# A two-layer hybrid trunk on one core: mixed keys copied one product ahead, projections spread evenly over the levels, LayerNorm sums from additions, activations written in place

## The chip, the cores and the metric

The kernel runs on one core of a Trainium2 chip. The metric is device time in microseconds, the median of several executions. A profile shows one execution: what each engine did and when. The engines are named PE (TensorE, matmul), DVE (VectorE), ACT (ScalarE), POOL (GpSimd) and SP (SyncE, which issues most DMAs). Each engine works through its own queue in order; semaphores hold an instruction until what it needs is done.

## The reference, cut to what matters

Two layers are run over 1152 tokens: 128 context tokens and 1024 latent tokens. Each sub-layer is modulated, its output is gated and added to the scaled input, and a LayerNorm follows.

```python
# layer 0: attention beside a short gated convolution, then ConvFFN
# layer 1: HGRN2, a gated linear recurrence in both directions, then ConvFFN
x = layer_norm(ALPHA * x + gate * sublayer(x * (1 + scale) + shift))

def _hgrn_mixer(h, w_in, lb, norm_g, w_out, s_fw, s_bw):
    q, i, g, f_fw, f_bw = split(h @ w_in, 5)             # 8 heads of 128
    f = lb + (1 - lb) * sigmoid(f_raw)                   # decay; k = 1 - f
    # S_t = diag(f_t) S_(t-1) + k_t v_t ; o_t = q_t S_t, forward and backward
    o = rms_norm(o_f + o_b, norm_g) * silu(g)
    return o @ w_out, S_f, S_b

def _conv_ffn(h, w_up, conv_w, w_down):
    u = _dwconv(h @ w_up, conv_w)
    a, gt = split(u, 2)
    return (silu(gt) * a) @ w_down                       # 1024 -> 2 x 2816 -> 1024
```

All of it is float32.

## The kernel before, in words

Every large product is made from three fp32r products (`mm3`, L91 to L93): each operand is split into a rounded part and a remainder. `wraw` loads a weight of 128 x 1024; `wsplit` makes `whi` on ScalarE (L106) and subtracts to get `wlo`, on GpSimd unless another engine is named (L107). Activations are kept the same way, feature rows by tokens, in `hT` (two tiles of four feature blocks for each part; `Halves`). The tokens are nine tiles of 128 (t = 8 down to 0) or three chunks of 384 (c = 2, 1, 0).

From the output projection of layer 0 on, the order on every engine is the order in which the program is written; only semaphores between engines move anything.

**Feed-forward.** `ffn_up` makes 44 products (tile `psu`) with a convolution behind each on ScalarE and VectorE (L973 to L979) and stores the result to DRAM. At the last one it splits the first two weights of the down phase (`dws`) and the first two loaded activations (`split_s`). `ffn_down` works in groups of four feature blocks. The last group is made for whole token tiles (`psw`, three buffers of two banks): gate (L1173), addition (L1174), `ln_stats` (two `bn_stats` of 512 columns, an aggregate, a power on GpSimd, a scaling pass on ScalarE), and what a `tail` function adds: `tail1` the two affine passes of the output (L267 on VectorE, L268 on GpSimd), `tail0` the transposition into the next layer's `hT` by `ln_out` (four pieces of two feature blocks for each chunk). `ln_sums`, used in the output projection of the recurrence so far, gets the mean from an addition that also sums and the variance from a square on ScalarE.

**Recurrence.** Head by head. Its projections (input i, gate g, two decays f, query q; 24 steps each, one step being the three products of one feature block with 384 tokens, tile `psp`) are a generator, `projections`, out of which `fill(n)` takes n steps wherever it is called, so that TensorE has work between the steps of the scan. ScalarE evacuates them. The scan is a tree of seven levels over three chunks, 21 items (`level`):

```python
km = wtile("km")
nc.scalar.copy(km..., scan_ap(X, KBF, KBB, c * 384, 384, hh))      # mixed keys
for q3 in range(3): mm(ps..., km..., scan_ap(X, QAB, QAF, c0, P, hh))
# X *= the neighbour's total: one half on GpSimd, one on VectorE (L1364)
# new totals (L1370); copy_predicated of ps into sT (L1372), both on VectorE
```

`X` holds keys and queries of both directions, four arrays over all tokens; a level multiplies it in place. After each `level`, `fill(4)` is called (3 in head 0, 2 in head 7). Then come the states (six `fill(2)`) and the outputs (`fill(4)` three times and `fill(8)`); `upto` completes a projection that is needed, and `at["last"]` holds `fill` back from running too far ahead. Head 7 has no next head: behind its last projection come `early` products, the first three heads' part of the output projection (`pse`), for which outputs of earlier heads are loaded from DRAM (`og_load`) and split (`og_split`, L1457 and L1458). `out_unit` splits the weights of the other five heads, and `recurrence_out` makes the rest (`psd`), with `ln_sums`; it also loads and splits the first two weights of the second feed-forward (`ffn_raws`, `ffn_splits`).

## Time and profile before

| | us |
|---|---|
| median of 3 runs | 3557.26 (3554.27 to 3560.13) |
| the profiled execution, its time | 3557.42 |
| the profiled execution, its span | 3555.6 |
| TensorE busy | 3293.2 |
| VectorE busy | 1927.1 |
| GpSimd busy | 1255.0 |
| ScalarE busy | 1130.9 |

The span is from the first to the last instruction; the time holds 1.8 us more. A busy row gives for each engine the time, the share of the span and the number of instructions. A row of the waits reads "who <- for whom: us in total, times, longest". A row of instruction groups reads "line, engine, operation, tiles written <- read, shape, count | busy us, mean ns of one | idle us before them <- what ended it". A row of the timeline begins with start and length in us.

### The profile page before, as it was taken

What the parts mean: (1) busy time and instruction counts of PE and PEld (TensorE: products, weight loads), DVE (VectorE), ACT (ScalarE), POOL (GpSimd) and SP (SyncE); (2) the same over time, 40 slices, a digit from 0 to 9 for tenths busy, and PEclk for the clock granted to TensorE, in tenths of its full rate; (3) what the DMA queues carried; (4) which work ended last, traced back from release to release, by engine and by line L of the source; (5) the groups of instructions that cost most, each with busy time, mean ns of one, the idle gap of its engine ahead of it and who ended that gap; (6) DMA issues with size and microseconds to landing.
All of it is one profiled execution on the core that took longest, in us unless ns stands there. A gap on an engine that the chain in (4) does not pass through costs nothing. (4 is left out here: it accounts for less than half of the span.)

```text
span 3555.6 us, 45061 instructions
## 1 busy us (share of the span) xinstructions
PE 3293.2 (93%) x18215; PEld 3033.1 (85%) x18215; DVE 1927.1 (54%) x2667; ACT 1130.9 (32%) x1845; POOL 1255.0 (35%) x833
## 2 busy tenths in 40 slices
PE   7999999999999999988988888888789999999995
PEld 6998887799999988778887888787679999998884
DVE  6787886489973233564445454555742222233358
ACT  4314985232222231134333333333233222224111
POOL 6711333244312121423444444434423431112144
PEclk9999999999999999999999999999899999999998
DMA  7151002245552232321101111111302222223231
GB/s 203 50 154 36 1 1 79 70 128 167 166 148 62 82 126 89 116 77 67 58 20 50 46 46 30 35 52 54 123 13 84 86 86 69 62 82 126 95 120 62
DMA packets 261393, 286.39 MB, mean 81 GB/s; under 512 B 18132, under 2 KB 198560, under 8 KB 261185
## 3 DMA queue, kind: packets, MB, share of 16 engines
q1 hardware_dynamic: 260384, 281.88, 25.9%
q8 instruction: 144, 2.36, 0.3%
q0 software_dynamic: 800, 1.63, 0.2%
q14 instruction: 65, 0.52, 0.0%
HBM read 228.45 MB, written 55.02 MB: 80 GB/s over the span
## 5 line engine op out<-in xcount | busy, mean ns | idle before, releaser
L107 POOL TENSOR_TENSOR wlo<-wraw,whi 128x1024 fp32r<-128x1024 f32 x199 | 489.1, 2461 | 1307.0 <-ACT whi L106 1273.6
L91 PE MATMUL psu<-h,whi 128*128 128x388 f32 (+1 forms) x1488 | 509.5, 343 | 18.5 <-ACT psd L243 11.2
L92 PE MATMUL psu<-h,whi 128*128 128x388 f32 (+1 forms) x1488 | 509.4, 342 | 2.9 <-POOL h L386 2.9
L93 PE MATMUL psu<-h,wlo 128*128 128x388 f32 (+1 forms) x1488 | 507.8, 341 | 0.0
L974 DVE SCALAR_TENSOR_TENSOR cv<-psu,fcw,cv 128x1158 f32<-128x1158 f32 x88 | 125.2, 1423 | 529.8 <-ACT cv L973 529.8
L91 PE MATMUL psp<-h,whi 128*128 128x384 f32 x960 | 354.5, 369 | 5.4 <-ACT h L293 4.6
L92 PE MATMUL psp<-h,whi 128*128 128x384 f32 x960 | 330.7, 345 | 2.1 <-POOL h L294 2.1
L93 PE MATMUL psp<-h,wlo 128*128 128x384 f32 x960 | 331.1, 345 | 0.0
L973 ACT ACTIVATE cv<-psu,fcw 128x1158 f32<-128x1158 f32 x88 | 108.1, 1229 | 695.2 <-PE psu L93 695.2
L91 PEld LDWEIGHTS psu<-h,whi 128*128 128x128 f32 x1488 | 282.1, 190 | 20.3 <-ACT psd L243 11.4
L106 ACT ACTIVATE whi<-wraw 128x1024 fp32r<-128x1024 f32 x206 | 215.5, 1050 | 253.5 <-PE psd L93 86.1
L1358 PE MATMUL pss<-X,km 128*128 128x128 f32 x1008 | 168.3, 306 | 131.2 <-ACT km L1355 121.3
L1358 PEld LDWEIGHTS pss<-X,km 128*128 128x128 f32 x1008 | 139.5, 200 | 172.4 <-ACT km L1355 143.5
L92 PEld LDWEIGHTS psu<-h,whi 128*128 128x128 f32 x1488 | 282.0, 190 | 4.4 <-POOL h L386 3.9
L93 PEld LDWEIGHTS psu<-h,wlo 128*128 128x128 f32 x1488 | 281.6, 189 | 0.0
L91 PE MATMUL psd<-whi,s 128*128 128x512 f32 x648 | 256.5, 396 | 5.9 <-DVE cv L975 5.9
L1364 POOL TENSOR_TENSOR X<-X,tot 128x384 f32<-128x384 f32 x144 | 177.3, 1232 | 237.7 <-PE pss L1358 212.6
L92 PE MATMUL psd<-wlo,s 128*128 128x512 f32 x648 | 256.4, 396 | 0.0
L93 PE MATMUL psd<-whi,s 128*128 128x512 f32 x648 | 256.3, 396 | 0.0
L170 DVE SCALAR_TENSOR_TENSOR macc<-mraw,sil,macc 128x512 f32<-128x512 f32 x280 | 228.9, 884 | 12.6 <-DMA mraw<-in_w_mod_dram 12.6
L1364 DVE TENSOR_TENSOR X<-X,tot 128x384 f32<-128x384 f32 x144 | 103.9, 722 | 217.2 <-PE pss L1358 128.6
L1135 DVE TENSOR_TENSOR y<-y,psd 128x512 f32<-128x512 f32 x144 | 98.7, 685 | 222.1 <-PE psd L93 222.1
(327 smaller groups left out, 7515.9 us busy)
## 6 DMA issues: line engine op xcount, KB each, us to landing
wraw<-in_ffn_w_up_dram SPq DMA_DIRECT2D x88, 512.0 KB, 5.1
mraw<-in_w_mod_dram SPq DMA_DIRECT2D x80, 512.0 KB, 3.8
sd<-cv SPq DMA_DIRECT2D x44, 579.0 KB, 4.3
sraw<-sd SPq DMA_DIRECT2D x44, 579.0 KB, 3.8
wraw<-in_ffn_w_down_dram SPq DMA_DIRECT2D x44, 512.0 KB, 4.6
wraw<-in_hgrn_w_in_dram SPq DMA_DIRECT2D x40, 512.0 KB, 3.9
wraw<-in_attn_w_in_dram SPq DMA_DIRECT2D x18, 512.0 KB, 3.9
xd<-y SPq DMA_DIRECT2D x18, 512.0 KB, 5.3
```

The costliest lines, as they stand in the source:

```text
L91: mm(ps, l[0], r[0], start=start, stop=False)
L92: mm(ps, l[0], r[1], start=False, stop=False)
L93: mm(ps, l[1], r[0], start=False, stop=stop)
L106: nc.scalar.activation(hi[:, :n], raw[:, :n], AF.Copy)
L107: (eng or nc.gpsimd).tensor_tensor(lo[:, :n], raw[:, :n], r32(hi[:, :n]), op=ALU.subtract)
L170: nc.vector.scalar_tensor_tensor(acc[:, cond, :], r, sil[:, cond, k:k + 1], acc[:, cond, :], op0=ALU.mult, op1=ALU.add)
L973: nc.scalar.activation(t3, ps[:, :, 1:1 + OW], AF.Copy, scale=cw[1])
L974: nc.vector.scalar_tensor_tensor(t3, ps[:, :, 0:OW], cw[0], t3, op0=ALU.mult, op1=ALU.add)
L1135: nc.vector.tensor_tensor(y[t][:, cols], y[t][:, cols], ps, op=ALU.add)
L1358: mm(ps[:, q3 * P:(q3 + 1) * P], km[:, q3 * P:(q3 + 1) * P], scan_ap(X, QAB, QAF, c0, P, hh), start=True, stop=True)
L1364: eng.tensor_tensor(x, x, t4[:, :, :, 1 - half].unsqueeze(3).to_broadcast([P, 2, nb, hh]), op=ALU.mult)
```

## The change

1. `level`'s copy becomes `mixed_keys`, called for item n + 1 before the product of item n.
2. The steps that are left until the next head's query (less the twelve of the states) are spread evenly over the 21 items; in head 7 those left of the last projection. `at["last"]` and the turns give way to a count of steps.
3. The projections' `wlo` is made on VectorE.
4. In head 7 three heads' outputs are loaded and split with the last projection, heads 3 to 6 between the outputs (`og_rest`, on GpSimd). `early` fills both halves of a token tile at once. Two more output weights are loaded ahead, and each later unit is split before four steps and not after three.
5. `ffn_down`'s last group takes `ln_sums`, whose end comes after the next tile's gate.
6. The next layer's `hT` takes its second half in the last group's own tile, written chunk by chunk; seven of twelve pieces of the transposition are put among the last products instead of four with a delay. The recurrence's first weights are loaded earlier and split at tiles 4, 2 and 0.
7. The first two down weights are split before the convolution of the last product but one. The first weights of the second feed-forward are loaded one tile earlier and split on VectorE behind the sums of tiles 1 and 0.

```diff
+                if n == N - 1:
+                    for u in range(2):
+                        dws[u] = wsplit(*raws.pop(N + u))
                 if n:
                     conv(n - 1)
...
-            for t in range(NT - 1, -1, -1):
-                ps = pw.tile([P, 2, 512], F32, tag="w", name="psw")
...
-                nc.vector.tensor_tensor(y[t], y[t], p2, op=ALU.add)
-                end = ln_stats(y[t], lp, True)
+            for t in range(NT - 1, -2, -1):
...
+                    nc.vector.tensor_tensor(p2, p2, rows[:, cond_of(t), :], op=ALU.mult)
+                if end:
+                    end()
+                if t >= 0:
+                    end = ln_sums(y[t], p2, lp)
                 for f in behind:
                     f()
-                end()
-                behind = tail(t, y, gb, x1_tile, lbank, lp, todo)
+                behind = tail(t + 1, y, gb, x1_tile, lbank, lp, todo) if t < NT - 1 else []
...
-            state["h"] = new_h(False)
+            state["h"] = tuple(Halves([hp.tile([P, 4, PW], F32R, tag=f"h{q}0", name=f"h{q}0"),
+                                       parts[len(FGROUPS) - 1][q].halves[0]]) for q in range(2))
...
-            todo += [lambda: None] * 3 + [lambda f=f: f(bank, tmp) for f in fs[:2]]
+            n = (0, 3, 4)[c]
+            later0.extend(fs[n:])
+            now = [lambda f=f: f(bank, tmp) for f in fs[:n]]
+            now[2:2] = [lambda: None] * (c == 2)
+            todo += now
...
-    y = ffn_down(0, xd[0], dw, tail0, {5: lambda: first_weights(0), 2: lambda: first_weights(1),
-                                       0: lambda: first_weights(2)})
+    y = ffn_down(0, xd[0], dw, tail0, {7: lambda: (first_raw(0), first_raw(1)), 4: lambda: first_split(0),
+                                       2: lambda: first_split(1), 0: lambda: first_split(2)})
...
+        def mixed_keys(self, lv, c):
+            km = self.km[lv, c] = wtile("km")
+            hh = 1 << lv
+            nc.scalar.copy(km.rearrange("p (n s r) -> p n s r", s=2, r=hh),
+                           scan_ap(self.X, KBF, KBB, c * 384, 384, hh))
+
         def level(self, lv, c):
...
-            km = wtile("km")
-            nc.scalar.copy(km.rearrange("p (n s r) -> p n s r", s=2, r=hh), scan_ap(X, KBF, KBB, c * 384, 384, hh))
+            km = self.km.pop((lv, c))
...
-        wts[n] = wsplit(*raws.pop(n))
+        wts[n] = wsplit(*raws.pop(n), eng=nc.vector)
...
-            for hf in range(2):
-                cols = slice(hf * 512, (hf + 1) * 512)
-                ps = pp.tile([P, 512], F32, tag="p", name="pse")
-                for h in range(EARLY):
-                    w = flat(wts[NS + h])
+            pss = [pp.tile([P, 512], F32, tag="p", name="pse") for _ in range(2)]
+            for h in range(EARLY):
+                w = flat(wts[NS + h])
+                for hf, ps in enumerate(pss):
+                    cols = slice(hf * 512, (hf + 1) * 512)
...
-        for lv in range(7):
-            for c in (2, 1, 0):
-                hd.level(lv, c)
-                fill(FILL["level"] - (h == 0) if h < 7 else 2)
-        if h:
-            upto(pi(h))
+        steps = end_of(pq(h + 1)) - 6 * FILL["state"] if nh else end_of(pg(7))
+        steps -= at["steps"]
+        items = [(lv, c) for lv in range(7) for c in (2, 1, 0)]
+        hd.mixed_keys(*items[0])
+        for n, e in enumerate(items):
+            if n < 20:
+                hd.mixed_keys(*items[n + 1])
+            hd.level(*e)
+            fill(steps * (n + 1) // 21 - steps * n // 21)
...
+        else:
+            for c in (2, 1, 0):
+                og_rest(c, 0)
         o2 = hd.output(2)
+        if not nh:
+            og_rest(2, 1)
...
     for h in range(EARLY, 8):
-        fill(3)
-        out_unit(h, raws.pop(h))
+        out_unit(h, oraws.pop(h))
+        fill(4)
...
-            if t == 1:
+            if t == 2:
                 ffn_raws(1)
...
-            if t == 0:
-                ffn_splits(1, 2)
...
             end = ln_sums(y[t], p2, wk)
+            if t < 2:
+                ffn_splits(1, 1, nc.vector)
```

More of the change, by code (lines that the diff above doesn't have):

```diff
@@ L1485, in build @@
     NS = len(seq)
-    at = {"n": 0, "turn": 0, "last": 0}
+    at = {"steps": 0}
     wts, raws = {}, {}
@@ L1508, in projections, with rest @@
                     raw_of(n + 3)
-            at["n"] = n + 1
-        late.append((at["turn"] + 8, lambda: split_of(NS + 2)))
+        def rest():
+            split_of(NS + 2)
+            for h in (EARLY, EARLY + 1):
+                oraws[h] = out_raw(h)
+        late.append((at["steps"] + 2, rest))
         yield from early()
@@ L1528, in build, with end_of @@
     todo = projections()
+    def end_of(e):
+        return 24 * (next(i for i, x in enumerate(seq) if x[0] == e[0]) + 1)
     def fill(n):
         for _ in range(n):
-            at["turn"] += 1
-            while late and late[0][0] <= at["turn"]:
-                late.pop(0)[1]()
-            if at["n"] <= at["last"]:
-                next(todo, None)
+            for job in [job for job in late if job[0] <= at["steps"]]:
+                late.remove(job)
+                job[1]()
+            at["steps"] += 1
+            next(todo, None)
     def upto(e):
-        n = next(i for i, x in enumerate(seq) if x[0] == e[0]) + 1
-        while at["n"] < n:
-            fill(1)
+        fill(max(0, end_of(e) - at["steps"]))
     def settle():
@@ L1555, in build @@
     evs = [ev for _, ev in (pq(0), pi(0), pf(0, 0))]
-    first = [chunk_steps(w0[a], evs[a], 2) for a in range(2)]
-    for a in range(2):
-        for _ in range(4):
-            next(first[a])
-    for f in later0[0]:
-        f(pst, tmp)
+    later0.pop(0)(pst, tmp)
     nc.vector.memset(one, 1.0)
@@ L1674, in build @@
         o1 = hd.output(1)
+        if not nh:
+            og_rest(1, 1)
         if nh:
```

78 lines of the change are left out of this document (39 added, 39 removed).

## The prediction, made before the changed kernel was run

> **What bounds the kernel now.** I read the page first (busy shares), then TensorE's waits, then busy time by stage, and last the order of instructions inside one head.
>
> ```profile
> PE 3293.2 (93%) x18215; PEld 3033.1 (85%) x18215; DVE 1927.1 (54%) x2667; ACT 1130.9 (32%) x1845; POOL 1255.0 (35%) x833
> ...
> PE pss L1358 <- ACT km L1355: 121.3, 103, 3.1
> PE psu L91 <- ACT psd L243: 11.2, 1, 11.2
> ...
> PE psd L91 <- DVE cv L975: 5.9, 2, 2.9
> ```
>
> TensorE is the bound: it is busy for 3293.2 of 3555.6 us, and a gain can only come out of the 262 us in which it idles. Nearly half of these, 121.3 us in 103 waits, lie before one product, the level product of the recurrence, which waits for ScalarE's copy of the mixed keys (tile km). Where they lie is told by the stages. The columns are length, then busy us (and instructions) of PE, PEld, DVE, ACT, POOL, then granted clock, DMA share, GB/s.
>
> ```profile
> 1644.50:1760.60 116.10, 99.57 (x620) 93.83 (x619) 59.89 (x98) 38.18 (x70) 54.53 (x38) 0.97 0.13 44
> ...
> 2340.85:2456.90 116.05, 99.78 (x627) 94.19 (x627) 58.40 (x95) 38.37 (x69) 48.94 (x34) 0.99 0.13 40
> ...
> 1992.70:2072.80 80.10, 65.23 (x381) 60.26 (x382) 44.43 (x63) 25.36 (x44) 36.63 (x26) 0.98 0.12 34
> 2072.80:2108.75 35.95, 34.55 (x248) 33.91 (x245) 14.00 (x32) 13.01 (x26) 12.04 (x9) 1.00 0.17 52
> ...
> 2456.90:2526.00 69.10, 43.75 (x220) 37.65 (x221) 52.51 (x64) 24.15 (x36) 43.72 (x27) 0.81 0.29 92
> 2526.00:2589.30 63.30, 54.27 (x270) 44.52 (x268) 42.18 (x80) 11.29 (x19) 8.24 (x5) 0.93 0.38 134
> 1569.00:1614.00 45.00, 35.22 (x198) 33.70 (x197) 17.71 (x30) 21.74 (x36) 12.41 (x10) 0.85 0.30 104
> 3523.80:3555.60 31.80, 0.00 (x0) 0.00 (x0) 24.04 (x27) 4.70 (x4) 12.42 (x7) 0.56 0.20 82
> ```
>
> Heads 0 to 6 are seven equal periods of 116 us (first and last shown). One head is cut in two: its 21 level items take 80.10 us with 14.9 us of idle TensorE, the states and outputs 35.95 us with 1.4. Then follow head 7's levels, its states and outputs with the early output products, the way from the first feed-forward's end into the recurrence, and the kernel's end, where TensorE has nothing left and VectorE works 24 of 31.8 us.
>
> **Heads 0 to 6: keys one product ahead.** Today ScalarE gets the copy after the evacuations of the projections that precede it, and the product stands behind the copy.
>
> ```profile
> 2007.04 1.41 POOL L1364 TENSOR_TENSOR X<-X,tot 128x384 f32<-128x384 f32 x1 [2.01 <-PE pss L1358]
> ...
> 2008.48 0.56 ACT L1355 COPY km<-X 128x384 f32<-128x384 f32 x1 [2.64 <-POOL X L1364]
> ...
> 2043.05 0.91 ACT L1355 COPY km<-X 128x384 f32<-128x384 f32 x2
> ...
> 2045.56 1.17 POOL L1364 TENSOR_TENSOR X<-X,tot 128x384 f32<-128x384 f32 x1
> ...
> 2046.35 0.34 PE L93 MATMUL psp<-h,wlo 128*128 128x384 f32 x1
> 2046.52 0.27 PE L1358 MATMUL pss<-X,km 128*128 128x128 f32 x1
> ```
>
> At level 1 a copy starts 0.03 us after GpSimd's multiply of the item just before (2007.04 + 1.41), though that one wrote other columns: the multiply of the same columns lies three items back. At level 4 two copies run back to back, the second before the multiply at 2045.56, and its product starts at 2046.52, before that multiply ends (2046.73). So on early levels a copy is held by its neighbour's multiply, on late ones only by ScalarE's queue. Moved ahead, copy n+1 stands before product n and can be held by multiply n-1 at most; the evacuations behind product n no longer stand before it. Durations in this head:
>
> ```profile
> L1364 POOL TENSOR_TENSOR X<-X,tot 128x384 f32<-128x384 f32 x18 | 22.1, 1228 | 31.4 <-PE pss L1358 27.6 <-issue 3.9
> L1358 PE MATMUL pss<-X,km 128*128 128x128 f32 x127 | 20.9, 300 | 17.2 <-ACT km L1355 15.8 <-issue 1.3
> ...
> L1370 DVE TENSOR_TENSOR tot<-tot 128x192 f32<-128x192 f32 (+4 forms) x15 | 14.1, 938 | 0.0
> L1372 DVE COPY_PREDICATED sT<-masks,pss 128x384 f32<-128x384 uint8 x21 | 12.2, 579 | 0.0
> L107 POOL TENSOR_TENSOR wlo<-wraw,whi 128x1024 fp32r<-128x1024 f32 x5 | 11.9, 2375 | 20.7 <-ACT whi L106 20.7
> L1355 ACT COPY km<-X 128x384 f32<-128x384 f32 x21 | 10.9, 535 | 16.8 <-POOL X L1364 16.8
> L106 ACT ACTIVATE whi<-wraw 128x1024 fp32r<-128x1024 f32 x5 | 5.2, 1047 | 0.0
> ...
> L1364 DVE TENSOR_TENSOR X<-X,fb 128x384 f32<-128x384 f32 x3 | 2.0, 666 | 6.5 <-PE pss L1358 6.5
> ```
>
> Without idle an item is 65.23 / 21 = 3.1 us of TensorE. Beside it VectorE needs 0.67 + 0.94 + 0.58 = 2.2, GpSimd 1.2, ScalarE 0.54 and an evacuation every second item: all below 3.1, so TensorE stays the bound. The 14.9 us go. So does the half-rate clock: 0.98 over 80.1 us is 1.6 us. Small extra: with no wait a product starts 0.17 us before its forerunner's modelled end (2046.52 against 2046.69), 12 times or 2.0 us. New on early levels: product n+1 can still be held by multiply n, if reads of X are tracked as coarsely as the copy's; product 1.0 (six of the 127 instructions in 20.9 us) + multiply 1.2 to 1.4 + hand-offs of 0.1 each is 2.4 to 2.6, just under 3.1, so I allow 1.7 us of stalls. Unseen, this costs between 0 and 5.4 us (12 early items at 0.45, a rival below); 1.7, as the level rows lie nearer to "fits". Net 14.9 + 1.6 + 2.0 - 1.7 = 16.8 us a head, 7 times **118 us**. The first copy of a head stays behind the diagonal's evacuation: its wait remains. Projections spread evenly (about 4.2 steps an item instead of 4 and a lump later) move 4 steps from the second part to the first: nothing, as both are full of TensorE work. The weights' subtractions go from POOL to VectorE, behind which multiplies, totals and masks then queue:
>
> ```profile
> L107 DVE TENSOR_TENSOR wlo<-wraw,whi x7: 1219/1840/3370, 581.6 to 2585.3; 128x1024 fp32r<-128x1024 f32 x7
> ```
>
> Five at 1.22 to 3.37 (median 1.84) are 9.2 us a head on an engine with 116 - 58 us free; price nothing while the three items of slack hold, all 9.2 without them.
>
> **Head 7.** Its 28 remaining steps spread over 21 items instead of filling 14. TensorE needs 43.75 us, VectorE 52.5, now swollen by GpSimd's three late subtractions:
>
> ```profile
> PE psm L1385 <- POOL X L1364: 4.9, 1, 4.9
> ...
> PE pse L91 <- DVE y L1525: 5.3, 4, 2.2
> PE psd L91 <- DVE y L1525: 3.8, 1, 3.8
> ...
> L1458 POOL TENSOR_TENSOR h<-h,h 128x1152 fp32r<-128x1152 f32 x3 | 9.4, 3134 | 0.0
> ...
> L1525 DVE TENSOR_TENSOR y<-y,pse 128x512 f32<-128x512 f32 x14 | 9.6, 688 | 0.5
> ```
>
> Those leave the levels, so VectorE bounds them at about 52.5 plus 2 of hand-over: 69.1 to 55, a gain of 14 (between 0 and 69.1 - 43.75 = 25). They come back between the outputs (six SP loads, ScalarE copies, 3.1 us on POOL each), beside VectorE's normalization: cost 0 to 9.4, I take 2. The early products now fill both halves of a tile at once, with two PSUM buffers: each half is evacuated by two passes of 0.69, so the next tile waits 2.76 less a step of 0.7 (three products of 512 columns, scaled from the 0.17 between the starts at 2046.35 and 2046.52 for 384), about 1.5 us where nothing stands between; five of nine borders, less part of the 5.3 there today: cost 2 (0 to 8). Loading units 3 and 4 early hides behind the projections. Net **10 us**.
>
> **Into the recurrence.** Today the second half of the activations waits for whole tiles:
>
> ```profile
> PE psp L91 <- ACT h L293: 4.6, 1, 4.6
> PE pss L278 <- DVE y L1174: 3.1, 1, 3.1
> PE psp L92 <- POOL h L294: 2.1, 1, 2.1
> ```
>
> In place, seven of twelve pieces fit among the last products. These 9.8 us go, and with them part of the slow clock (0.85 over 45 us: 6.8 us, about half of it while TensorE worked). Late next is token tile 0: behind its last product stand multiply, sum, square, then the third weight's whi (1.05) and wlo (2.4) ahead of its power on POOL, and the scaling pass. I estimate 1.2 + 1.2 + 1.3, the power of the tile before with its hand-offs 0.9, 1.05 + 2.4, then 0.5 + 1.2 and 0.7 of hand-offs: 10.5 us. Ten projection steps of 0.5 and one piece's transposes cover 6 of them: 4.5 stay. Net 9.8 + 3.5 - 4.5 = **9 us** (4 to 13, from a tail that hides to one that costs twice).
>
> **LayerNorm sums and the end.**
>
> ```profile
> L232 DVE SCALAR_TENSOR_TENSOR bmv<-bmv 128x1 f32<-128x1 f32 x9 | 18.8, 2086 | 4.2 <-POOL bmv L229 4.2
> L226 DVE BATCH_NORM_STATS2 bst<-y 128x6 f32<-128x512 f32 x18 | 11.6, 685 | 0.3
> ...
> L1174 DVE TENSOR_TENSOR y<-y,psw 128x1024 f32<-128x1024 f32 x9 | 11.0, 1221 | 0.3
> ...
> L241 DVE SCALAR_TENSOR_TENSOR y<-psd,y 128x1024 f32<-128x1024 f32 x9 | 11.0, 1218 | 0.0
> L243 ACT ACTIVATE psd<-y,bmv 128x1024 f32<-128x1024 f32 x9 | 10.1, 1119 | 16.2 <-DVE bmv L242 15.6
> ```
>
> Of the nine tiles VectorE is 31.8 us late at the end. It loses two statistics of 0.685 a tile and most of L232's 2.09 (a 128x1 operation that stands beside GpSimd's affine pass); the add (1.22) becomes an add with sum (1.22), and the square (1.12) goes to ScalarE. From 8.1 us a tile it comes to about 5, below TensorE's 5.5 (24 products of 512 columns at 0.23, scaled as above). ScalarE gets the square beside its scaling pass, 2.4 of 5.5, and is free otherwise. So only one tile's tail is left. I estimate it by the rows: multiply, waiting power, sum and square 4.7; the power behind a GpSimd affine pass of 2.4 and the scaling, 4.2; the last two affine passes, the second half on POOL, 5: some 14 us, and 3.3 for the last store as today: 17.3 against 31.8, and 1.5 for a product that is held today: **16 us** (10 to 20: a tail 6 longer or 4 shorter).
>
> **Small ones.** Before the second feed-forward, the power of the last tile stands behind two subtractions of 2.4 on POOL: 4.8 of the 11.2 us go, VectorE's own subtraction returns 1.5: **3 us** (0 to 5). The two down-weight splits, moved ahead of a convolution, gain nothing: what is waited for there (5.9 us, two times) is the last convolution's own VectorE pass.
>
> Sum: 118 + 10 + 9 + 16 + 3 = 156; 3555.6 - 156 = 3399.6, and 1.8 around the span (the profiled run took 3557.4, 0.2 over the median): **3401 us**, by itself 3380 to 3425.
>
> [...]
>
> **The rivals.**
> - *Multiply chain.* On levels 0 to 3 product n+1 waits for multiply n, and that for copy n+1, which ScalarE runs late behind evacuations: 0.45 us on 12 items, 5.4 a head less the 1.7 allowed. Against it: 2.4 to 2.6 is under 3.1. 3401 + 7 x 3.7 = 3427; with twice the price 3465. Chance 0.18.
> - *VectorE's subtractions.* A subtraction and a GpSimd multiply that read at once hold each other up: median 1.84 against 1.22. If none hides, 9.2 x 7 = 64: 3465. Against it: three items of slack. Chance 0.10. [...]
> - *The copy does not hold the product.* If the multiply does, levels keep their time: 3401 + 118 = 3519. For it: the copy starts 0.03 us after the multiply. Chance 0.06.
> - *Slower.* A copy held by a multiply blocks the evacuations queued behind it on ScalarE; two projection buffers fill and TensorE stops in the filling. Product 1.0, multiply 1.4, copy 0.55, an evacuation of two such passes 1.1 and hand-offs 0.2 in a row are 4.3 us an item against 80.1 / 21 = 3.81; on 147 items +72, less the other 38: 3591. It decides from 4.07 an item. Chance 0.05.
>
> The forecast has 0.55; better than 3380 (no stall, all bounds good) 0.06. The range 3368 to 3458 leaves out some 0.2: the far cases and the upper half of the middle ones. Changes under 0.2% (7 us) can't be told from none: faster 0.93, same 0.02, slower 0.05.
>
> **What would show it.** The wait of L1358 for km falls from 121 to about 20 us (first items and head 7), a head's period to 99 us, wlo of the projections is on VectorE at under 2 us; head 7's levels take 55; the last product ends under 20 us before the end; the waits of L293 and L294 are gone. Wrong if L1358 instead waits for X, or the evacuations come late.

## The result, and the profile after

The changed kernel takes 3391.57 us (median of four runs, 3387.23 to 3395.16) where the kernel before, run beside it, takes 3555.77. The ratio is 0.9536 with a 95% interval of 0.9519 to 0.9554, so 164 us or 4.6% went. 3401 had been forecast, with a range of 3368 to 3458. The profiled run of the changed kernel took 3387.23, with a span of 3385.4.

The first part of its page, busy time and share of the span by engine:

```profile
PE 3244.5 (96%) x18215; PEld 3015.4 (89%) x18215; DVE 1891.2 (56%) x2690; ACT 1156.7 (34%) x1884; POOL 1153.0 (34%) x795
```

TensorE is still the bound, now at 96%. Of the 262 us in which it idled 141 are left, and its busy time fell too, from 3293.2 to 3244.5 with the same 18215 matmuls. Next, TensorE's waits in the changed kernel (us in total, times, longest). The level product is L1373 now, its copy L1362, the multiply L1379:

```profile
PE pse L91 <- DVE y L1550: 14.0, 11, 4.0
PE pss L1373 <- ACT km L1362: 10.6, 12, 1.1
PE pss L1373 <- POOL X L1379: 9.6, 13, 1.7
...
PE pss L278 <- ACT psw L243: 7.7, 1, 7.7
...
PE psl L278 <- ACT y L249: 7.0, 2, 6.3
PE psu L91 <- ACT psd L243: 6.8, 1, 6.8
```

The wait for the mixed keys fell from 121.3 us to 10.6. The wait of the early projections for a free bank grew from 5.3 us to 14.0; new are 7.7 and 6.3 us before two groups of transposes on the way into the recurrence.

Where the time went is seen when both traces are cut at the same events. In order: the first feed-forward's last pass up to head 0's first level product; heads 0 to 6; head 7's levels up to its flips; from there to the last output projections; these up to the second feed-forward's first product; and, far later, the last pass up to the end. Busy time by stage, before:

```profile
1513.30:1650.12 136.82, 121.54 (x622) 108.32 (x622) 67.99 (x105) 53.81 (x78) 38.83 (x29) 0.94 0.26 86
1650.12:2456.89 806.77, 695.66 (x4349) 656.86 (x4350) 406.59 (x665) 266.36 (x479) 349.10 (x241) 0.98 0.13 40
2456.89:2519.54 62.65, 42.24 (x214) 36.54 (x215) 46.05 (x58) 23.66 (x35) 38.19 (x25) 0.85 0.32 101
2519.54:2589.34 69.80, 55.78 (x275) 45.66 (x275) 48.64 (x85) 11.78 (x20) 13.77 (x8) 0.89 0.34 122
2589.34:2670.74 81.40, 70.07 (x319) 56.52 (x319) 30.43 (x73) 34.73 (x44) 21.14 (x18) 0.94 0.05 14
3470.22:3555.64 85.42, 52.19 (x216) 41.51 (x216) 70.12 (x76) 11.17 (x9) 36.35 (x21) 0.82 0.15 59
```

The same six stages after, then the level items of one head (3), and the tail behind the last product:

```profile
1510.04:1648.76 138.72, 121.20 (x621) 108.88 (x622) 49.67 (x98) 65.16 (x96) 32.90 (x27) 0.94 0.26 84
1648.76:2317.09 668.33, 656.36 (x4347) 648.25 (x4347) 424.95 (x699) 268.37 (x480) 272.98 (x207) 1.00 0.16 49
2317.09:2360.78 43.69, 33.61 (x213) 29.45 (x214) 40.41 (x61) 16.28 (x28) 26.19 (x21) 1.00 0.27 86
2360.78:2436.07 75.29, 58.62 (x280) 45.37 (x278) 50.60 (x85) 19.62 (x30) 19.09 (x12) 0.93 0.41 148
2436.07:2513.35 77.28, 69.11 (x319) 55.34 (x319) 30.95 (x65) 33.74 (x44) 16.54 (x16) 0.98 0.06 21
3315.26:3385.43 70.17, 52.04 (x216) 41.67 (x216) 41.20 (x67) 22.38 (x27) 29.34 (x21) 0.86 0.18 72
...
1932.02:1992.03 60.01, 59.75 (x379) 59.25 (x380) 44.00 (x64) 25.28 (x43) 26.41 (x20) 1.00 0.15 46
3367.30:3385.43 18.13, 0.00 (x1) 0.00 (x0) 8.71 (x13) 3.72 (x4) 8.84 (x6) 0.57 0.28 116
```

Read the first number of each row against its partner. Heads 0 to 6 give 138.4 us and head 7's levels 19.0; the early projections take 5.5 back; the second feed-forward starts 4.1 sooner; the last pass and the tail give 15.3. The way into the recurrence, from which 9 us were expected, got 1.9 longer. In head 3's levels TensorE now idles 0.26 us of 60.01, against 14.9 of 80.10 before. Of the 138.4 us of the seven heads 99.1 are idle time (111.1 to 12.0) and 39.3 are busy time. Some 15.4 of these are slow clock: in the heads of the kernel before, the clock was granted at half rate (0.50) in nine stretches of 3.41 us, after the change in none. The other 23.9 fit products that don't wait and so start before the modelled end of the one ahead (0.17 us in the prediction's rows, 2046.52 against 2046.69). The run keys_late below agrees: at a clock of 1.00, with the copy late, TensorE is busy 23.6 us longer (679.94 against 656.36).

Rows of the changed kernel's timeline at a level border in head 3 (start, us):

```profile
1941.69 1.00 PE L1373 MATMUL pss<-X,km 128*128 128x128 f32 x6
...
1942.28 0.55 ACT L1362 COPY km<-X 128x384 f32<-128x384 f32 x1
...
1942.91 1.41 POOL L1379 TENSOR_TENSOR X<-X,tot 128x384 f32<-128x384 f32 x1 [1.68 <-ACT km L1362]
...
1944.35 0.56 ACT L1362 COPY km<-X 128x384 f32<-128x384 f32 x1 [1.52 <-POOL X L1379]
...
1944.63 0.90 PE L1373 MATMUL pss<-X,km 128*128 128x128 f32 x6
```

This is the chain that was feared: the multiply waits for the next item's copy (ends 1942.83, starts 1942.91), the copy after it for that multiply (ends 1944.32, starts 1944.35). But the product at 1944.63 needs only the copy that ended at 1942.83. Its distance to the product before, 2.94 us, is filled by TensorE's own work.

### The profile page after: what moved, and what is told of

Same layout as the page of the kernel before. It is cut to its first block, busy times and chain, and to the rows that moved or that the text cites. A ratio compares the mean times of both kernels' runs of the same rounds, so it can differ in the third digit from the quotient of the medians.

```text
span 3385.4 us, 45066 instructions
## 1 busy us (share of the span) xinstructions
PE 3244.5 (96%) x18215; PEld 3015.4 (89%) x18215; DVE 1891.2 (56%) x2690; ACT 1156.7 (34%) x1884; POOL 1153.0 (34%) x795
## 5 line engine op out<-in xcount | busy, mean ns | idle before, releaser
L107 POOL TENSOR_TENSOR wlo<-wraw,whi 128x1024 fp32r<-128x1024 f32 x158 | 388.1, 2460 | 1169.7 <-ACT whi L106 1161.1
L91 PE MATMUL psu<-h,whi 128*128 128x388 f32 (+1 forms) x960 | 329.5, 344 | 15.4 <-DVE sc L597 7.5
L92 PE MATMUL psu<-h,whi 128*128 128x388 f32 (+1 forms) x960 | 329.7, 343 | 2.2 <-POOL h L386 2.2
L93 PE MATMUL psu<-h,wlo 128*128 128x388 f32 (+1 forms) x960 | 327.8, 341 | 0.0
L1379 POOL TENSOR_TENSOR X<-X,tot 128x384 f32<-128x384 f32 x144 | 182.3, 1266 | 214.0 <-PE pss L1373 112.1
L91 PEld LDWEIGHTS psu<-h,whi 128*128 128x128 f32 x960 | 182.3, 190 | 17.1 <-issue 8.2
L92 PEld LDWEIGHTS psu<-h,whi 128*128 128x128 f32 x960 | 182.3, 190 | 3.7 <-POOL h L386 3.2
L91 PE MATMUL psu<-ra,whi 128*128 128x388 f32 x528 | 181.1, 343 | 2.9 <-DVE y L909 2.7
L93 PEld LDWEIGHTS psu<-h,wlo 128*128 128x128 f32 x960 | 182.0, 190 | 0.0
L92 PE MATMUL psu<-ra,whi 128*128 128x388 f32 x528 | 179.8, 341 | 0.0
L93 PE MATMUL psu<-rb,wlo 128*128 128x388 f32 x528 | 179.7, 340 | 0.0
L93 PE MATMUL psu<-s,wlo 128*128 128x388 f32 x528 | 179.7, 340 | 0.0
L93 PE MATMUL psu<-ra,wlo 128*128 128x388 f32 x528 | 179.6, 340 | 0.0
L92 PE MATMUL psu<-rb,whi 128*128 128x388 f32 x528 | 179.5, 340 | 0.0
```

The costliest lines, as they stand in the source:

```text
L91: mm(ps, l[0], r[0], start=start, stop=False)
L92: mm(ps, l[0], r[1], start=False, stop=False)
L93: mm(ps, l[1], r[0], start=False, stop=stop)
L107: (eng or nc.gpsimd).tensor_tensor(lo[:, :n], raw[:, :n], r32(hi[:, :n]), op=ALU.subtract)
L1379: eng.tensor_tensor(x, x, t4[:, :, :, 1 - half].unsqueeze(3).to_broadcast([P, 2, nb, hh]), op=ALU.mult)
```

## The experiments: heads 0 to 6

Four kernels take the change's parts for the heads asunder: the copy ahead, the projections' subtractions on VectorE, and the even spreading of projection steps.

**The copy alone taken back** (keys_late): the changed kernel, each copy issued right before its own product.

```diff
-        hd.mixed_keys(*items[0])
...
-            if n < 20:
-                hd.mixed_keys(*items[n + 1])
+            hd.mixed_keys(*e)
             hd.level(*e)
```

> The changed kernel with one thing undone: the copy of the mixed keys is called right before its own product again; even spreading and subtractions on VectorE stay. Theory 'order' (what held the product was the copy's place in ScalarE's queue): the period of heads 1 to 6 goes from 96.3 back to 112 to 116 us, the wait of the level product for km back to 14 or more a head, the whole to 3510 to 3540 us. Rival 'subtraction' (GpSimd's subtractions held the multiplies, and their move to VectorE gave most): the period stays under 104, the whole under 3450.

It took 3507.89 us. Heads 0 to 6 by stage, and the wait in them:

```profile
1652.76:2417.79 765.03, 679.94 (x4346) 643.29 (x4347) 431.36 (x699) 267.35 (x479) 270.62 (x207) 1.00 0.14 43
```

```profile
PE pss L1373 <- ACT km L1362: 79.7, 75, 1.7
```

765.03 against 668.33: the order of the copy is worth 96.7 us here. The period of heads 1 to 6, 109.7 us, lies between the two theories, and the wait, 11.4 us a head, is below the 14 expected: the order explains most of the gain, but 41.7 us of it (806.77 to 765.03) come without the copy.

**The copy alone done** (keys_only): the kernel before with the copy one product ahead and nothing else.

```diff
-                hd.level(lv, c)
-                fill(FILL["level"] - (h == 0) if h < 7 else 2)
+        hd.mixed_keys(*items[0])
+        for n, e in enumerate(items):
+            if n < 20:
+                hd.mixed_keys(*items[n + 1])
+            hd.level(*e)
+            fill(FILL["level"] - (h == 0) if h < 7 else 2)
```

> The kernel before with one part of the change alone: the copy one product ahead. Theory 'order': the period falls from 116 to 96.5 to 99, head 7's levels from 62.6 to 48 to 58, the whole to 3415 to 3435 us. Rival 'subtraction': subtractions still sit on GpSimd, so the period falls to 103 to 110 only and the whole stays above 3455.

It took 3451.05 us. Heads 0 to 6, head 7's levels, and what stands first among the waits in heads 0 to 6:

```profile
1647.15:2354.90 707.75, 674.21 (x4350) 662.43 (x4350) 405.34 (x665) 267.55 (x480) 342.37 (x241) 0.98 0.15 46
2354.90:2405.50 50.60, 37.78 (x214) 33.72 (x215) 46.43 (x57) 23.27 (x35) 35.95 (x25) 0.92 0.40 125
```

```profile
PE pss L1364 <- POOL X L1370: 23.7, 14, 1.9
```

The copy alone gives 99.0 us, not 118: the period of heads 1 to 6 is 102.4 us where 96.5 to 99 was expected, and it and the time lie between the two theories, nearer to the rival's 103 and 3455. What stops it is the rival's mechanism, a late multiply: twice a head the product waits 1.7 us for GpSimd's multiply, and the clock stays at 0.98.

**The subtractions back on GpSimd** (wlo_pool): the changed kernel but for one argument.

```diff
-        wts[n] = wsplit(*raws.pop(n), eng=nc.vector)
+        wts[n] = wsplit(*raws.pop(n))
```

> The changed kernel with the projections' subtractions on GpSimd again (2.4 us each, five a head). Theory 'order': they hold a multiply now and then, 0 to 2 us a head, so the period of heads 1 to 6 is 96 to 98.5 and the whole 3385 to 3405. Rival 'subtraction': five times most of 2.4 come back, the period is 103 to 108, the whole 3435 to 3475.

It took 3415.12 us. Heads 0 to 6 by stage; then, from the timeline of head 3, why a product waits:

```profile
1656.00:2340.94 684.94, 663.57 (x4347) 654.78 (x4347) 439.84 (x665) 268.57 (x480) 346.24 (x241) 0.99 0.16 48
```

```profile
1967.11 2.39 POOL L107 TENSOR_TENSOR wlo<-wraw,whi 128x1024 fp32r<-128x1024 f32 x1 [1.68 <-ACT whi L106]
1969.45 1.22 POOL L1379 TENSOR_TENSOR X<-X,tot 128x384 f32<-128x384 f32 x1
...
1970.72 0.94 PE L1373 MATMUL pss<-X,km 128*128 128x128 f32 x6 [1.87 <-POOL X L1379]
```

The heads are 16.6 us longer than in the changed kernel, 2.4 a head. The period of heads 1 to 6, 99.0 us against 96.3, misses the range of the order's theory by 0.5 us, and the time misses it by 10. Not all of these 10 belong to the edit: the heads begin 7.2 us later than in the changed kernel's first profile (1656.00 against 1648.76), and in its second profile, of the same kernel, they begin 4.9 us later too. The multiply stands behind a subtraction of 2.39 us in GpSimd's queue, and the product starts 0.05 us after the multiply ends. So the slack of three items that the dependency allows is not there when the multiply comes late: the next product, of other columns, is held too. On VectorE, in the changed kernel, the subtractions of head 3 are cheap, and GpSimd's multiplies hardly longer on average (1.29 us against 1.23 before). Groups of head 3: busy us and mean ns of one, then the idle time before them:

```profile
L1379 POOL TENSOR_TENSOR X<-X,tot 128x384 f32<-128x384 f32 x18 | 23.1, 1285 | 29.0 <-PE pss L1373 14.7 <-ACT km L1362 8.4 <-issue 3.7
...
L107 DVE TENSOR_TENSOR wlo<-wraw,whi 128x1024 fp32r<-128x1024 f32 x5 | 6.4, 1282 | 3.4 <-ACT whi L106 3.4
```

**The lumps back** (bunched): the changed kernel with four steps an item and the rest in a lump in heads 0 to 6, two an item in head 7.

```diff
-            fill(steps * (n + 1) // 21 - steps * n // 21)
+            fill((4 if h else 3) if nh else min(2, max(0, steps - 2 * n)))
```

> The changed kernel with the steps bunched as before: 4 an item (3 in head 0), the rest in one lump before the outputs, and 2 an item in head 7 until they are used up. Theory 'order': TensorE has the same work, so the period of heads 1 to 6 changes by less than 1 us; head 7's levels, 42.8 us, grow by 3 to 10, as the last 7 items have nothing beside their chain of product and multiply. Rival 'spread' (the even spreading keeps the product out of the multiply's reach): the period grows by 3 or more.

It took 3386.95 us; heads 0 to 6 and head 7's levels:

```profile
1649.36:2315.11 665.75, 655.50 (x4347) 648.32 (x4347) 439.85 (x699) 267.39 (x480) 269.84 (x207) 1.00 0.16 49
2315.11:2359.78 44.67, 34.85 (x216) 31.84 (x216) 39.12 (x58) 16.80 (x29) 24.61 (x20) 0.96 0.28 89
```

Even spreading costs 2.6 us in heads 0 to 6 and saves 1.0 in head 7: next to nothing. For head 7's levels 3 to 10 had been expected; that missed. The four runs and the two kernels together, heads 0 to 6 in us:

| | copy late | copy ahead |
|---|---|---|
| subtractions on GpSimd, lumps | 806.8 (before) | 707.8 (keys_only) |
| subtractions on GpSimd, even | not run | 684.9 (wlo_pool) |
| subtractions on VectorE, lumps | not run | 665.8 (bunched) |
| subtractions on VectorE, even | 765.0 (keys_late) | 668.3 (changed) |

The copy is worth 97 to 99 us either way. Moving the subtractions is worth 42.0 us with lumps and 16.6 with even spreading, and even spreading 22.8 us with the subtractions on GpSimd and -2.6 without. That neither adds to the other fits one cause for both, a multiply that comes late. The first row is the kernel before without the rest of the change, the others are the changed kernel, so 42.0 and 22.8 contain whatever else differs between the two in these heads.

## The experiments: the way into the recurrence

Four kernels look for what took the 9 us. The last tiles of the pass in the changed kernel's timeline:

```profile
1578.43 1.80 POOL L294 TENSOR_TENSOR s<-ht,s 128x768 fp32r<-128x768 f32 x1 [4.31 <-ACT s L293]
...
1580.19 0.54 POOL L247 TENSOR_TENSOR bmv<-bmv,mhalf 128x1 f32<-128x1 f32 x1
...
1580.84 1.22 DVE L241 SCALAR_TENSOR_TENSOR y<-psw,y 128x1024 f32<-128x1024 f32 x1
...
1582.35 1.12 ACT L243 ACTIVATE psw<-y,bmv 128x1024 f32<-128x1024 f32 x1
...
1583.64 0.69 PE L278 MATMUL pss<-ident,y 128*128 128x128 f32 x2 [7.74 <-ACT psw L243]
```

The power for token tile 1's normalisation (L247) stands behind a subtraction on GpSimd, tile 0's addition (L241) behind that power in VectorE's order, the Square (L243) behind the addition, and it holds the PSUM bank in which TensorE's next transposes are to be put. TensorE idles 7.74 us.

**First weights on VectorE** (first_vec), to take GpSimd's queue away:

```diff
-        w0[n] = wsplit(*w0[n])
+        w0[n] = wsplit(*w0[n], eng=nc.vector)
```

> The changed kernel with one edit: the first recurrence weights' remainders are subtracted on VectorE again. Theory 'GpSimd's queue': in the transition (first recurrence weights to head 0, 138.7 us against 136.8 before the change) TensorE's waits of 6.3 and 7.7 us come from GpSimd doing the first weights' subtraction ahead of the LayerNorm's power; then the transition falls to 130 to 133 us and the rest stays within 1 us. Rival 'PSUM bank': the 7.7 us wait is the Square's hold on the bank alone, and VectorE, with the addition 1.2 us later, gives back what GpSimd saves: 137 to 140 us.

**Square into SBUF** (sq_sbuf), to free the bank earlier:

```diff
-        nc.scalar.activation(p2, z, AF.Square, bias=mv[:, 1:2], accum_out=mv[:, 2:3])
+        sq = small.tile([P, D], F32, tag="lsq", bufs=1, name="lsq")
+        nc.scalar.activation(sq, z, AF.Square, bias=mv[:, 1:2], accum_out=mv[:, 2:3])
```

> The changed kernel with the Square of the LayerNorm's sums written to a scratch tile in SBUF instead of the PSUM bank. Theory 'bank': the bank comes free about 1.2 us earlier after each token tile's last addition; the waits of 7.7 and 6.8 us for ScalarE's Square shrink by 1 to 2 us each, 2 to 4 us in all. Rival 'chain': what is late there is the addition before the Square, and nothing changes within 1 us.

**Addition ahead of the power** (add_first):

```diff
-                if end:
-                    end()
+                prev = end
                 if t >= 0:
                     end = ln_sums(y[t], p2, lp)
+                if prev:
+                    prev()
```

> The changed kernel with two lines exchanged in the down phase's last pass: a token tile's addition, sum and Square are issued ahead of the end of the tile before it, so VectorE does not wait for GpSimd's power before it adds. Theory 'queue': the 7.7 us wait for the PSUM bank falls to 3 to 5 us, as the addition of token tile 0 stood behind the power of tile 1; the wait for the normalised tile (6.3) moves by no more than 1.5 either way; the transition falls from 138.7 to 134 to 137. From the last product to the end, 18.1 us become 17 to 20. Rival 'chain': the tiles are normalised 1.4 us later each, and what the bank gains the transposes lose: 138 to 141.

**The last pass as before** (ln_old): statistics passes and normalisation in the tile's own turn, in both layers, the rest of the change kept.

```diff
...
-                if end:
-                    end()
-                if t >= 0:
-                    end = ln_sums(y[t], p2, lp)
...
+                nc.vector.tensor_tensor(y[t], y[t], p2, op=ALU.add)
+                end = ln_stats(y[t], lp, True)
                 for f in behind:
                     f()
-                behind = tail(t + 1, y, gb, x1_tile, lbank, lp, todo) if t < NT - 1 else []
+                end()
+                behind = tail(t, y, gb, x1_tile, lbank, lp, todo)
...
+            now[0:0] = [lambda: None] * 2
```

The last line puts two empty places ahead of the pieces of the transposition, which so stay where the change has them.

> The changed kernel with the down phases' last pass as it was before: the statistics passes over the finished token tile, and each tile's normalisation issued in its own turn, in both layers; the rest of the change stays. Theory 'a turn late': the transition (first product of the last pass to head 0's first level, 138.7 us changed, 136.8 before) is long because a tile is normalised behind the next tile's multiply, and transposes wait 6.3 and 7.7 us for that; it falls to 126 to 132, while the time from the last product to the end goes back from 18.1 to 31 to 32 us and the last pass with it (85 us from first product to end, against 70). Rival 'order': the waits come from what else moved in the transition (weights' subtractions, transposed chunks); then it stays at 136 to 140 and only the end is given back.

The times were 3392.44, 3391.92, 3394.13 and 3404.26 us. By stage, from the pass's first product to head 0; first first_vec, sq_sbuf and add_first:

```profile
1512.36:1652.24 139.88, 121.78 (x621) 109.09 (x622) 53.78 (x101) 65.15 (x96) 25.82 (x24) 0.93 0.25 83
```

```profile
1511.45:1649.95 138.50, 121.98 (x621) 109.71 (x621) 50.01 (x98) 65.12 (x96) 32.88 (x27) 0.93 0.25 84
```

```profile
1513.88:1655.32 141.44, 124.25 (x621) 111.70 (x622) 50.71 (x98) 64.65 (x96) 32.88 (x27) 0.92 0.25 82
```

And ln_old, with its stage at the kernel's end:

```profile
1512.21:1647.78 135.57, 122.39 (x622) 109.23 (x622) 64.35 (x107) 53.75 (x78) 32.97 (x27) 0.95 0.26 85
3315.75:3402.20 86.45, 53.52 (x216) 42.50 (x216) 69.99 (x76) 11.18 (x9) 36.36 (x21) 0.80 0.15 59
```

These lengths hold the granted clock, which differs between runs (last section). The first number less PE's busy time is free of most of that (the changed kernel's two profiles, at 0.94 and 0.90, give 17.5 and 17.9): 15.3 us before, 17.5 changed, 18.1 first_vec, 16.5 sq_sbuf, 17.2 add_first, 13.2 ln_old.

First_vec's theory fell: without the weights' subtractions on GpSimd the idle time is no smaller. It didn't clear the whole queue, though: the subtraction of the rows above, of a transposed piece (L294), stands ahead of that power there too (1.80 us from 1581.86, the power at 1583.62). The bank is a small part: with the Square elsewhere, in sq_sbuf, the waits before those transposes and before the second feed-forward are 6.3 and 5.5 us, 1.4 and 1.3 less, as its theory had it, and they end with the addition now. In add_first, whose addition no longer stands behind the power, the first of these waits is 4.5, as its theory had it, but those before the other transposes grew from 7.0 to 9.6 us, and at 141.44 the stage is no shorter: its rival came true, by which the transposes lose what the bank gains.

Ln_old, which normalises a tile before the next tile's multiply, is the only one that brings much back: 4.3 us of idle time (3.1 of length). Its theory had asked for 7 to 13 us of length, so the late turn is a part of what is missing here and not all of it. Since the run takes back sums and turn together, it can't tell the two apart. It also gives back the end: 86.45 against 70.17 us, with 69.99 us of VectorE instead of 41.20. The change does the same thing in both places; at the end it pays, here it doesn't.

## The experiments: the early projections, and a version of the parts

**One half after the other** (early_old): the early projections as before.

```diff
-        late.append((at["steps"] + 2, rest))
+        late.append((at["steps"], rest))
...
-            pss = [pp.tile([P, 512], F32, tag="p", name="pse") for _ in range(2)]
-            for h in range(EARLY):
-                w = flat(wts[NS + h])
-                for hf, ps in enumerate(pss):
-                    cols = slice(hf * 512, (hf + 1) * 512)
+            for hf in range(2):
+                cols = slice(hf * 512, (hf + 1) * 512)
+                ps = pp.tile([P, 512], F32, tag="p", name="pse")
+                for h in range(EARLY):
+                    w = flat(wts[NS + h])
```

> The changed kernel with the early projections (after head 7's flips) filled one half after the other again, and the last head's even spreading kept. Theory 'early': waits for the projection bank (14.0 us in 11 waits) come from filling both halves together; they fall to 5 to 10 us and the stretch from the flips to the next states from 76.2 to 70 to 73. Rival 'subtractions': the waits come from the gated output's subtractions on GpSimd beside VectorE; then the stretch stays at 75 to 77.

**Gated output on VectorE** (og_vec):

```diff
-                og_split(c, a, n, nc.gpsimd)
+                og_split(c, a, n, nc.vector)
```

> The changed kernel with the gated output's subtractions on VectorE instead of GpSimd. Theory 'subtractions': the 4.0 and 3.2 us stalls in the early projections go, and the stretch from the flips to the states falls from 76.2 to 70 to 72. Rival 'early': it stays at 75 to 77, as the order of the two halves makes the waits.

They took 3391.72 and 3394.78 us. From the flips to the last output projections, in early_old:

```profile
2369.00:2439.30 70.30, 57.06 (x279) 46.59 (x278) 49.78 (x85) 19.50 (x30) 19.15 (x12) 0.93 0.44 158
```

Filling both halves at once costs 5.0 us (75.29 to 70.30). Which engine does the gated output's subtractions costs nothing: with them on VectorE the stage takes 76.10 us. Of the 5.0 us, 1.5 went again in the next stage (78.76 against 77.28), at a clock of 0.94 instead of 0.98: the same instructions, slower.

**The parts together** (best3): the changed kernel with ln_old's pass in the first layer alone, the lumps in heads 0 to 6, the early projections one half after the other, and the Square in SBUF; beside it the changed kernel again.

> The changed kernel with four edits that the runs point to: the down phase's last pass of the first layer with statistics passes in the tile's own turn (transition -3.1 us), projection steps in equal lumps in heads 0 to 6 (-3.0), the early projections one half after the other (-5.0 in that stretch, of which 1.5 were given back by half-rate clock windows), the Square written to SBUF (-1.4 at the second FFN's down phase). If the parts add up: 10 to 12 us under the changed kernel beside it, 3375 to 3382 us. If windows of half clock move in where waits go, as they did in three of the runs: 3382 to 3390.

> The changed kernel once more on the same chip, as the measure for the version with four edits: 3385 to 3396 us, as its runs so far lie.

Medians of five and four runs: 3378.83 us (3373.78 to 3383.60) and 3391.85 (3389.65 to 3393.13). The ratios to the kernel before are 0.9508 (0.9495 to 0.9521) and 0.9538 (0.9525 to 0.9551): the intervals do not meet, and the version is 13.0 us faster than the changed kernel. Its way into the recurrence, heads 0 to 6 and early projections:

```profile
1509.95:1645.05 135.10, 122.91 (x622) 109.98 (x622) 64.05 (x107) 53.75 (x78) 33.00 (x27) 0.94 0.26 86
...
1645.05:2310.74 665.69, 655.45 (x4346) 648.24 (x4346) 439.81 (x699) 267.37 (x480) 269.86 (x207) 1.00 0.16 49
...
2354.44:2424.26 69.82, 55.36 (x279) 45.01 (x278) 49.74 (x85) 19.51 (x30) 19.15 (x12) 0.95 0.45 160
```

Against the changed kernel's first profile 3.6, 2.6 and 5.5 us less: the three parts are there side by side. The fourth, the Square in SBUF, made the wait before the second feed-forward 1.4 us shorter (5.4 against 6.8), but its stage is no shorter (77.42 against 77.28), at a clock of 0.96 instead of 0.98.

## Why the prediction was right, and where it wasn't

The large term had the right cause. That the time came within 10 us is also luck: the heads gave 20 us more than was put, and misses the other way took much of that back; the profiled run, the fastest of the four, is 14 us off. In spans (3555.64 to 3385.43, 170.2 us, where 156 had been forecast), by the steps of the prediction; head 7 is divided as the prediction divided it, behind the first flips, and so its two rows differ from the stages above:

| term | predicted | measured |
|---|---|---|
| heads 0 to 6 | 118 | 138.4 |
| head 7's levels | 14 | 24.2 |
| early projections and gated output | -4 | -10.7 |
| into the recurrence | 9 | -1.9 |
| the end | 16 | 15.3 |
| start of the second feed-forward | 3 | 4.1 |
| all else | 0 | 0.8 |

Head 7's levels in that window, after the change (the row before, of 69.10 us, stands in the prediction):

```profile
2317.09:2362.07 44.98, 34.59 (x220) 30.19 (x221) 41.70 (x64) 17.36 (x31) 26.28 (x21) 1.00 0.28 89
```

- **What bounds it.** "A gain can only come out of the 262 us in which it idles" was too narrow: 48.7 of the 170 us are busy time that went (3293.2 to 3244.5). The sum itself had counted some of it, as slow clock and early starts.
- **Heads 0 to 6.** "The 14.9 us go" was right: 14.6 of head 3's items. In the terms of the sum, a head gained 14.2 us of idle time where 14.9 less 1.7 had been put, 2.2 of slow clock where 1.6 had, and 3.4 of early starts where 2.0 had. The "small extra" of the early starts is so the most undersized of the three, 10 of the 20 us. Two steps failed as to where this comes from, with opposite signs. The stalls that the copy would meet on the multiply, put at 1.7 us a head, are 3.4 if the copy is moved alone (keys_only: 23.7 us over seven heads), so the copy itself gives 99 us. And the subtractions' move, "price nothing", was the remedy for just that: with the even spreading and the rest of the change it brings 39.4 us (707.8 to 668.3), and the stalls shrink with it, to 2.4 us in these seven heads. I had asked what five subtractions cost on VectorE and not what GpSimd's multiplies gain when nothing of 2.4 us stands before them. On VectorE they took 1.28 us each, not the 1.84 of the price, a median of seven passes from all over the trace of before.
- **The rivals of the heads.** The multiply chain exists (the timeline above, and keys_only with 3.4 us a head, between the 1.7 allowed and the 5.4 of its worst); in the changed kernel the wait for it is 9.6 us in all, head 7 included. VectorE's subtractions and GpSimd's multiplies did lengthen each other where they met, as the second rival had it (in head 3 a multiply of 1.80 us against 0.86, a subtraction of 1.55 against 1.22; last section), but the level products waited for the multiply only 2.4 us in the seven heads. The slower case stayed away: an item takes 60.01 / 21 = 2.86 us, far from the 4.07 at which it would decide.
- **The clock.** 1.6 us a head were put for slow clock, from the 0.98 of head 3's levels. The trace of after bears this out: 1.00 in the seven heads, 0.98 before, where no wait in these heads was longer than 2.2 us. But it isn't the number of waits: keys_late has 75 of them for the copy in these heads, and its clock is 1.00. The last section shows what stood ahead of the slow stretches.
- **Head 7's levels.** Under-sized: in the prediction's own window, 69.1 us before, they take 45.0 us, not 55. The bound of VectorE was wrong: it was busy 41.70 us here, not 52.5. The prediction called the 52.5 us swollen by GpSimd's late subtractions and still took them as the floor; in the change, where those are gone, VectorE's same 18 multiplies took 0.79 us each instead of 1.03. Of the levels without the flips, 62.65 us before, the copy alone leaves 50.60 (keys_only), the whole change 43.69; what else brought those 6.9 us no run separates.
- **Early projections.** Both costs were under-sized. Both halves at once cost 5.0 us where 2 had been put; the prediction's own working, 2.76 less a step of 0.7, gives 2.1 us a border and not the 1.5 it went on with. The other 5.7 us stand against the 2 put for the gated output's passes. That early_old's stage (70.30) is hardly longer than the one before (69.80) doesn't speak against this, as the one before holds 4.9 us of waiting for GpSimd's multiply ahead of the flips, and that wait is gone. Where the 5.7 us come from, no run separates; the engine of the subtractions it is not (og_vec).
- **Into the recurrence.** The step that failed is "these 9.8 us go ... 4.5 stay". The old waits did go. But token tile 0 kept TensorE 7.7 us, and a second wait of 6.3 was not in the sum: every tile is normalised a turn later now, and token tile 3's transposes come to wait for it. The slow clock did not come back either (0.94 and 0.94). Without the late turn (ln_old) the stage is 1.3 us shorter than before, so even then most of the 9 us is missing; its waits have other names but the idle time is 13.2 against 15.3. Why so little of the pieces' move shows, no run here separates.
- **The end, and the second feed-forward.** Right in size, and at the end in cause: 17.3 us had been estimated for the tail, 18.13 were measured, and ln_old, which takes back the sums with their turn, gives it back. VectorE's 8.1 us a tile was 7.8 by the stage (70.12 over nine tiles), and 4.6 after. Before the second feed-forward the wait fell from 11.2 us to 6.8, by 4.4 where the working gave 3.3; no run tests the cause given for it.

## What to carry to other kernels

When an operand's copy is issued ahead, ask what else the next consumer waits for: here the copy gave 99 us, and another 39 came when the multiply next in line no longer came late. Taking the long subtractions out of its queue did that (42 us with lumps), even spreading did a part of it (23 us), and the two don't add up. An edit that is priced at nothing on the engine it moves to may still pay on the one it leaves. And a step that defers work by one turn pays where nothing waits for the turn and costs where something does; the same code was worth 16 us in one place and cost 3 in another, as ln_old shows.

## What the runs showed of the hardware

The granted clock differs between runs of the same kernel. The changed kernel on the way into the recurrence, in its second profile:

```profile
1510.30:1653.65 143.35, 125.42 (x622) 112.52 (x622) 50.53 (x98) 65.19 (x96) 32.86 (x27) 0.90 0.24 81
```

It idles 17.9 us, much as in the first (17.5), but the stage is 4.6 us longer at a clock of 0.90 instead of 0.94. Spans of 3385.4 and 3391.0 for one kernel come mostly from this, and single runs that differ by less than some 6 us say little by their time; idle time and waits told the edits apart where the times didn't.

What stood ahead of the slow stretches can be read from the traces. In heads 0 to 6 of the kernel before, the clock was granted at 0.50 in nine stretches of 3.41 us and at 1.00 in the rest; in those of the changed kernel it was granted at 1.00 throughout. One of the nine, behind the 3.41 us ahead of it; then 3.41 us out of the heads of keys_late:

```profile
1947.37:1950.78 3.41, 1.26 (x10) 1.20 (x10) 0.17 (x1) 2.54 (x5) 1.57 (x1) 1.00 0.00 0
1950.78:1954.19 3.41, 3.41 (x13) 3.41 (x12) 2.43 (x3) 0.00 (x0) 1.91 (x2) 0.50 0.00 0
```

```profile
2026.80:2030.21 3.41, 1.69 (x13) 1.51 (x12) 1.74 (x4) 2.19 (x4) 0.34 (x1) 1.00 0.00 0
```

In the first row TensorE was busy for 1.26 of 3.41 us, and half rate followed; ahead of all nine it was busy for 1.17 to 1.60, and ahead of eight of them the idle time is one wait of 1.81 to 2.24 us for the copy. Five more waits of 2.2 us (the first ends at 1927.62) had no slow stretch behind them. In the heads of the changed kernel no wait is longer than 1.1 us, and no 3.41 us hold less than 2.27 of TensorE's work (from 1832.34 us). In the row of keys_late it was busy for 1.69 us; there and over its seven heads the clock was 1.00, in spite of 75 waits for the copy, none of them longer than 1.7 us. So the length of the waits tells these kernels apart and their number doesn't; what sets the clock, and why it differs between runs of one kernel, was not shown.

Second, GpSimd's subtraction of 128x1024 took 2.39 us (wlo_pool) and VectorE's 1.28 on average (changed kernel) in head 3. Some took longer where the other engine was at work. In head 3 of the changed kernel:

```profile
1989.27 1.22 DVE L107 TENSOR_TENSOR wlo<-wraw,whi 128x1024 fp32r<-128x1024 f32 x1 [0.91 <-ACT whi L106]
...
1989.40 1.80 POOL L1379 TENSOR_TENSOR X<-X,tot 128x384 f32<-128x384 f32 x1 [1.56 <-PE pss L1373]
```

This multiply, begun 0.13 us behind VectorE's subtraction, took 1.80 us and ended 0.71 us after it. At 1972.24 a multiply that began 0.40 us ahead of the next subtraction took 0.86 us, and that subtraction 1.55 instead of 1.22. In the kernel before, five of VectorE's seven subtractions were long, 1.54 to 3.37 us; each of them began while a GpSimd one of about 2.4 us ran, and the two that met none took 1.22 and 1.23. So the delay of the two engines that I had feared is there, but beside short multiplies it is small: their mean rose by 0.06 us, from 1.23 to 1.29.
